# A hybrid decoder block on one core: activations stationary and weights moving in all large products

## The chip, the core and the metric

The kernel runs on one core of a Trainium2 chip, in one launch. The metric is device time in microseconds, the median of three runs: before 1590.8 us (1589.44 to 1592.45). Engines are named as the profile names them: PE is TensorE (PEld its loads of stationary operands), DVE VectorE, ACT ScalarE, POOL GpSimd, SP the engine that issues most transfers.

## The reference, cut to what matters

256 tokens, 2048 channels, float32. Six modulation vectors come from one matrix, the input is normalized and modulated, projected by one wide matrix, mixed by a gated delta rule (8 heads of 128) and by a convolution of width 31, merged by two sigmoid gates and projected out; then a gated MLP (5632 wide) with a convolution of width 3 on its gate.

```python
mod = silu(c) @ w_ada + b_ada                      # 2048 x 12288
sh1, sc1, gt1, sh2, sc2, gt2 = split(mod, 6)
hn = rmsnorm(x, norm1_g) * (1 + sc1) + sh1
proj = hn @ w_in                                   # qkv, z, beta, a, glu, gate_a, gate_b
a = delta_rule(silu(conv4(qkv)), beta, g) * silu(z) @ dn_w_o
b = silu(layernorm(conv31(val * sigmoid(gl)))) @ cf_w_o
x = x + gt1 * ((sigmoid(gate_a) * a + sigmoid(gate_b) * b) @ w_out)
hn = rmsnorm(x, norm2_g) * (1 + sc2) + sh2
gate, up = split(hn @ w_up, 2)
x = x + gt2 * ((silu(conv3(gate)) * up) @ w_down)
out = rmsnorm(x, final_norm_g)
```

## The kernel before

Channels lie on the partitions throughout: x is fed transposed, and `x_sb`, `hn`, `gb`, `ga`, `mg`, `res` are 16 row tiles of 128 channels by 256 tokens. All large products go through `product` (L257): for 512 outputs, two banks of sums, and for each pair of row tiles a weight chunk `w` of 2 x 128 x 512 (512 KB). ScalarE rounds it to a leading part `wh` (L267), VectorE makes the remainder `wl` (L269); activations are split the same way, and three matmuls make up one product: `wh` by the leading part (L280), `wh` by the rest (L281), `wl` by the leading part (L282). The weights are stationary in blocks of 128x128, the 256 tokens move: 24 matmuls a chunk. `w` has five buffers, `wh` and `wl` three. There are 488 chunks.

The order of products: `p1` (70 chunks: the first rows for q, k, v, GLU and a gate), the last rows of these, z, gate `ga`, the convolution branch's `cfo` (16), the delta branch's `dno` (16), `out` (32), `up1` (60: the first rows of six groups of the MLP), then the rest of gate and up, `down` (48), five more groups of gate and up, `down` (40).

The modulation vectors are side work (`ada_block`, L134). A step brings 384 or 512 KB of `w_ada` into `ada_w` and VectorE adds the rows, each times an entry of silu(c), to `ada_acc` (L155). A block of 8 or 16 steps ends with sums over the partitions (turns on TensorE, L172). `product` pulls steps as it issues chunks, `side_rate` of them per chunk; from L768 on `ada_w` has two buffers. `need` (L194) pulls all steps that are left of a block: the first output gate before `out` (L819), scale and shift of the second norm before `up1` (L829) and inside it (L840).

The order of instructions on an engine comes from a scheduler that simulates the program, with priorities in bands (`b_first` before `b_delta`, `b_w`, `b_main`, `b_ada`). Each engine then runs its list in order. PSUM: four banks `mm` for products, one `sm`, three (`dl`, `dl0`, `dl1`) for the delta rule and the rest. The delta rule's state `St` (L602) and Q of the first heads (L423) have buffers of their own.

Of the kernel before, what the change touches and what calls it, by code (L numbers as in the profile page):

```python
# [8 lines left out]
F32 = mybir.dt.float32  # L9
# [20 lines left out]
for _name, _w in (  # L30
    ("b_ada", 96), ("n1g", 16), ("n2g", 16), ("fg", 16), ("dnconv", 96), ("dng", 1),
    ("cfconv", 248), ("lng", 8), ("lnb", 8), ("ffconv", 132), ("c", 16),
):
    VEC[_name] = (_n, _w)
    _n += _w
# [3 lines left out]
class Band:  # L39
    """A run of scheduling priorities of its own."""  # L40
# [15 lines left out]
def block_kernel(ctx: ExitStack, tc, xT, vec, ab, w_ada, w_in, dn_w_o, cf_w_o, w_out, w_up, w_down, outT):  # L56
# [61 lines left out]
    R3, R2 = [(0, 4), (4, 10), (10, KD)], [(0, 8), (8, KD)]  # L118
    RANGES = [R3, R3, R2, R3, R3, R2]
    mod = [[p0.tile([P, k1 - k0], F32, name=f"mod{j}{k0}") for k0, k1 in RANGES[j]] for j in range(6)]  # L120
# [13 lines left out]
    def ada_block(j, part, pool, bufs, band=None, shared=False):  # L134
# [3 lines left out]
        acc = (pool if shared else p0).tile([P, n if shared else 1024], F32, tag="ada_acc", bufs=2 if shared else 1, name="ada_acc")  # L138
        c0 = j * D + k0 * P
        step = 2 if n <= 512 else 1  # L140
        if shared:
            pt = ps.tile([P, 512], F32, tag="sm", name="pt")
        for kc in range(0, KD, step):
            with band():
                wt = pool.tile([P, step, n], F32, tag="ada_w", bufs=bufs, name="ada_w")
                last_ada[0] = nc.sync.dma_start(out=wt, in_=av[:, kc:kc + step, c0:c0 + n]).ins
                for i in range(step):
# [4 lines left out]
                    elif k == 0:  # L152
# [3 lines left out]
            if kc + step < KD:  # L156
                yield
        with (b_delta if band is not nullcontext else nullcontext)():
            if band is nullcontext:
                if not shared:  # L160
                    pt = ps.tile([P, 512], F32, tag="sm", name="pt")
# [3 lines left out]
            else:  # L165
                # the sums over the partitions, with the channels turned to the partitions
                tot = p0.tile([P, nk], F32, tag="ada_t", name="ada_t")
                for i in range(0, nk, 4):
                    n4 = min(4, nk - i)
                    pt = ps.tile([P, 4, P], F32, tag="sm", name="pt")  # L170
# [33 lines left out]
    def sumsq_acc(acc, src, k, pt):  # L204
        """Adds src ** 2 / D over the channels to pt[:, c] for the tokens of chunk c, with most of the sums over the row tiles on the vector engine."""
        n = KD - 4
        sq = acc if k == 0 else p0.tile([P, 2, S], F32, tag="t2", bufs=2, name="sq1")[:, 0, :]
        nc.scalar.activation(out=sq, in_=src, func=AF.Square)
        if 0 < k < n:
            nc.vector.tensor_tensor(out=acc, in0=acc, in1=sq, op=ALU.add)  # L210
        if k >= n - 1:
            v = acc if k == n - 1 else sq
            for c in range(2):
                nc.tensor.matmul(pt[:, c:c + 1], lhsT=v[:, c * P:(c + 1) * P], rhs=ones_d, start=(k == n - 1 and c == 0), stop=(k == KD - 1), skip_group_check=True)
# [7 lines left out]
    def spread(a, pool=pd, tag="dl"):  # L222
        """a ** -0.5 of two columns, as rows on every partition."""
# [17 lines left out]
    def modulate(dst, src, A, sh, rs, part):  # L241
        """dst[:, 0] and dst[:, 1]: the leading part and the rest of src * A * rstd + sh."""
# [704 lines left out]
```

## Time and profile before

| | |
|---|---|
| median of three runs | 1590.8 us |
| span of the profiled execution | 1586.7 us |
| its instructions | 31357 |
| busy: TensorE, VectorE, ScalarE | 1545.4, 1188.0, 796.2 us |
| transfers | 366.25 MB, mean 231 GB/s |

The median is the time of an execution, the span lies inside it, from the first to the last instruction of the profile; what the profiled execution itself took beside its span is not recorded, and the two differ by 4.1 us. In the page, a duration of a matmul contains the time that it waits in the pipeline behind others: how far apart two starts lie (the pitch) says what a matmul costs in a stream. The chain of waits is read backwards from the last instruction. Windows give the busy time of each engine in a stretch, and the clock granted to TensorE there (1.00 is 2.4 GHz, 0.50 is 1.2 GHz).

### The profile page before, as it was taken

To read this page: it belongs to the slowest core of one execution; us is meant where nothing else is said; L and a number is where in the kernel's file an instruction comes from. 1 tells how busy PE (TensorE), PEld (TensorE's weight loads), DVE (VectorE), ACT (ScalarE), POOL (GpSimd) and SP (SyncE) were. 2 spreads that over 40 slices of the span, in tenths; PEclk is the share of its full clock that TensorE was granted. 3 is DMA by queue.
4 is the path that set the end of the run, shared out by engine and by line. 5 is a ranking of instruction groups with operands and counts; after the bars stand their busy time and mean duration, and the time that the engine had idled before them with its cause. 6 is when DMAs were issued, how large, how long until landed. Compare 5 with 4: busy or idle time off the path is not lost.

```text
span 1586.7 us, 31357 instructions
## 1 busy us (share of the span) xinstructions
PE 1545.4 (97%) x12818; PEld 1534.9 (97%) x12818; DVE 1188.0 (75%) x1566; ACT 796.2 (50%) x1232; POOL 51.7 (3%) x112
## 2 busy tenths in 40 slices
PE   6999999899999999999989999999999999999997
PEld 5999999899999999999979999999999999999997
DVE  5789967789889878897777889987444777655554
ACT  4554434766885584454446434555334444444443
POOL 2000000400020010000000000000000000000000
PEclk7999999999999999999989999999999999999998
DMA  9999866534456668889779998765556777665552
GB/s 346 384 335 349 266 185 174 159 107 131 122 155 218 199 192 303 305 271 340 254 241 305 308 307 305 216 183 184 187 189 224 244 253 262 190 185 185 187 187 94
DMA packets 186848, 366.25 MB, mean 231 GB/s; under 512 B 12496, under 2 KB 37072, under 8 KB 186704
## 3 DMA queue, kind: packets, MB, share of 16 engines
q1 hardware_dynamic: 186704, 364.26, 70.1%
q8 instruction: 100, 1.64, 0.4%
q14 instruction: 44, 0.36, 0.1%
HBM read 362.11 MB, written 2.10 MB: 230 GB/s over the span
## 4 chain that ended last, share of the span: by engine, by line
PE 86%; DMA 5%; DVE 3%; issue 2%; POOL 2%; ACT 1%; SPq 0%; DVEq 0%; POOLq 0%; ACTq 0%
PE mm_up L282 7%; PE mm_up L280 7%; PE mm_up L281 7%; PE mm_down L282 5%; PE mm_down L280 5%; PE mm_down L281 5%; DMA ada_w<-in_w_ada 5%; PE mm_p L282 4%; PE mm_p L281 4%; PE mm_p L280 4%; PE mm_gate L280 4%; PE mm_gate L281 4%; PE mm_gate L282 4%; PE mm_ga L282 2%; PE mm_ga L281 2%; PE mm_ga L280 2%
## 5 line engine op out<-in xcount | busy, mean ns | idle before, releaser
L267 ACT CAST wh<-w 128x1024 fp32r<-128x1024 f32 x488 | 511.4, 1049 | 631.0 <-PE mm_up L281 141.0
L269 DVE TENSOR_TENSOR wl<-w,wh 128x1024 fp32r<-128x1024 f32 x488 | 595.5, 1221 | 265.0 <-ACT wh L267 263.8
L155 DVE SCALAR_TENSOR_TENSOR ada_acc<-ada_w,c_act,ada_acc 128x768 f32<-128x768 f32 (+2 forms) x232 | 237.6, 1024 | 65.2 <-DMA ada_w<-in_w_ada 62.8
L280 PE MATMUL mm_up<-hn,wh 128*128 128x256 f32 x944 | 266.4, 285 | 1.7 <-ACT hn L251 1.7
L281 PE MATMUL mm_up<-hn,wh 128*128 128x256 f32 x944 | 267.4, 284 | 0.0
L282 PE MATMUL mm_up<-hn,wl 128*128 128x256 f32 x944 | 264.7, 284 | 0.2 <-DVE wl L269 0.2
L282 PE MATMUL mm_down<-h,wl 128*128 128x256 f32 x704 | 197.5, 281 | 0.0
L280 PE MATMUL mm_down<-h,wh 128*128 128x256 f32 x704 | 197.0, 280 | 0.0
L281 PE MATMUL mm_down<-h,wh 128*128 128x256 f32 x704 | 195.8, 278 | 0.0
L280 PEld LDWEIGHTS mm_up<-hn,wh 128*128 128x128 f32 x944 | 181.9, 193 | 2.0 <-ACT hn L251 2.0
L281 PEld LDWEIGHTS mm_up<-hn,wh 128*128 128x128 f32 x944 | 182.1, 193 | 0.0
L282 PEld LDWEIGHTS mm_up<-hn,wl 128*128 128x128 f32 x944 | 180.7, 193 | 0.4 <-DVE wl L269 0.4
L280 PE MATMUL mm_p<-hn,wh 128*128 128x256 f32 x560 | 157.1, 285 | 1.6 <-ACT hn L251 1.6
L281 PE MATMUL mm_p<-hn,wh 128*128 128x256 f32 x560 | 157.7, 285 | 0.3 <-DVE hn L252 0.3
L282 PE MATMUL mm_p<-hn,wl 128*128 128x256 f32 x560 | 153.1, 286 | 0.1
L281 PEld LDWEIGHTS mm_down<-h,wh 128*128 128x128 f32 x704 | 132.4, 188 | 0.0
L280 PEld LDWEIGHTS mm_down<-h,wh 128*128 128x128 f32 x704 | 132.4, 188 | 0.0
L282 PEld LDWEIGHTS mm_down<-h,wl 128*128 128x128 f32 x704 | 132.1, 188 | 0.0
L281 PE MATMUL mm_gate<-hn,wh 128*128 128x256 f32 x464 | 131.0, 283 | 0.0
L280 PE MATMUL mm_gate<-hn,wh 128*128 128x256 f32 x464 | 130.9, 283 | 0.0
L282 PE MATMUL mm_gate<-hn,wl 128*128 128x256 f32 x464 | 129.7, 283 | 0.0
L280 PEld LDWEIGHTS mm_p<-hn,wh 128*128 128x128 f32 x560 | 108.2, 194 | 1.6 <-ACT hn L251 1.6
(301 smaller groups left out, 3334.0 us busy)
## 6 DMA issues: line engine op xcount, KB each, us to landing
w<-in_w_up SPq DMA_DIRECT2D x176, 512.0 KB, 4.4
w<-in_w_in SPq DMA_DIRECT2D x130, 512.0 KB, 3.9
ada_w<-in_w_ada SPq DMA_DIRECT2D x96, 512.0 KB, 5.2
ada_w<-in_w_ada SPq DMA_DIRECT2D x128, 384.0 KB, 5.2
w<-in_w_down SPq DMA_DIRECT2D x88, 512.0 KB, 3.7
w<-in_w_in SPq DMA_DIRECT2D x64, 256.0 KB, 4.1
w<-in_w_out SPq DMA_DIRECT2D x32, 512.0 KB, 5.1
w<-in_cf_w_o SPq DMA_DIRECT2D x16, 512.0 KB, 5.3
```

The costliest lines, as they stand in the source:

```text
L155: nc.vector.scalar_tensor_tensor(out=acc[:, 0:n], in0=wt[:, i, :], scalar=c_act[:, k:k + 1], in1=acc[:, 0:n], op0=ALU.mult, op1=ALU.add)
L267: nc.scalar.copy(out=wh, in_=w)
L269: nc.vector.tensor_tensor(out=wl, in0=w, in1=wh.bitcast(F32), op=ALU.subtract)
L280: nc.tensor.matmul(o, lhsT=wh[:, kk, cs], rhs=xh(k), start=(k == k0 and j % 2 == 0), stop=False, skip_group_check=True)
L281: nc.tensor.matmul(o, lhsT=wh[:, kk, cs], rhs=xl(k), start=False, stop=False, skip_group_check=True)
L282: nc.tensor.matmul(o, lhsT=wl[:, kk, cs], rhs=xh(k), start=False, stop=(k == k1 - 1), skip_group_check=True)
```

## The change

In `product` the activations become the stationary operand, 128 tokens at a time, and 512 columns of a weight chunk move: 12 matmuls a chunk. Sums then lie with tokens on the partitions, [128 tokens, 512 outputs] in each of two banks. Where channels must be on the partitions (convolutions, merged branches, normalized input, the MLP's hidden values) a new helper `turned` transposes two row tiles by four turns into a bank of tag `tp` (two banks). x and the output are no longer transposed outside; norms sum squares along a row on ScalarE (`add_to_res`, `rstd_col`). The two output gates become rows on all partitions, by a matmul with ones (`as_row`); their bias comes in as a row by a transfer, after a clearing on POOL. Q of the first heads (`conv00`) and the state `St` move into the buffers of `ada_w`. Cut to its core, with the removed code of the evictions left out:

```diff
-    ps = ctx.enter_context(tc.tile_pool(name="ps", bufs=1, space=bass.MemoryType.PSUM))
+    ps = ctx.enter_context(tc.tile_pool(name="ps", bufs=2, space=bass.MemoryType.PSUM))
...
+        as_row = j in (2, 5)
+        if as_row:
+            with (b_delta if band is not nullcontext else nullcontext)():
+                nc.gpsimd.memset(acc, 0.0)
+                r0 = (j == 5) * D + k0 * P
+                nc.sync.dma_start(out=acc[0:1, 0:n], in_=rowv[:, r0:r0 + n])
...
+        if as_row:
+            with b_delta():
+                for i in range(0, n, 512):
+                    pt = ps.tile([P, 512], F32, tag="tp", name="pt")
+                    nc.tensor.matmul(pt, lhsT=ones, rhs=acc[:, i:i + 512], start=True, stop=True)
+                    nc.scalar.copy(out=gt_row(j, (k0 * P + i) // 512), in_=pt)
+            ready.add((j, part))
+            yield
+            return
...
+    def rstd_col(ss):
+        a = p0.tile([P, 2], F32, tag="nrm_a", name="nrm_a")
+        nc.vector.tensor_reduce(out=a, in_=ss, axis=mybir.AxisListType.X, op=ALU.add)
+        nc.gpsimd.tensor_scalar(out=a, in0=a, scalar1=1.0 / D, scalar2=EPS, op0=ALU.mult, op1=ALU.add)
+        r = p0.tile([P, 2], F32, tag="nrm_c", bufs=3, name="nrm_c")
+        nc.gpsimd.tensor_tensor(out=r, in0=a, in1=mhalf[:, 0:2], op=ALU.pow)
+        return r
...
+    def turned(src, tiles, pool=ps, tag="tp"):
+        bank = pool.tile([P, 2, S], F32, tag=tag, name="turned")
+        for i, j in enumerate(tiles):
+            for t in range(2):
+                turn(bank[:, i, t * P:(t + 1) * P], src[:, t, j * P:(j + 1) * P])
+        return bank
...
-            order = [(kk, j) for kk in range(2) for j in range(4)] if kc + 2 < k1 else [(kk, j) for j in range(4) for kk in range(2)]
-            for kk, j in order:
+            order = [(kk, t) for kk in range(2) for t in range(2)] if kc + 2 < k1 else [(kk, t) for t in range(2) for kk in range(2)]
+            for kk, t in order:
                 k = kc + kk
-                o = pts[j // 2][:, j % 2, :]
-                cs = slice(j * P, (j + 1) * P)
-                nc.tensor.matmul(o, lhsT=wh[:, kk, cs], rhs=xh(k), start=(k == k0 and j % 2 == 0), stop=False, skip_group_check=True)
-                nc.tensor.matmul(o, lhsT=wh[:, kk, cs], rhs=xl(k), start=False, stop=False, skip_group_check=True)
-                nc.tensor.matmul(o, lhsT=wl[:, kk, cs], rhs=xh(k), start=False, stop=(k == k1 - 1), skip_group_check=True)
+                ts = slice(t * P, (t + 1) * P)
+                nc.tensor.matmul(pts[t], lhsT=xh(k)[:, ts], rhs=wh[:, kk, :], start=(k == k0), stop=False)
+                nc.tensor.matmul(pts[t], lhsT=xl(k)[:, ts], rhs=wh[:, kk, :], start=False, stop=False)
+                nc.tensor.matmul(pts[t], lhsT=xh(k)[:, ts], rhs=wl[:, kk, :], start=False, stop=(k == k1 - 1))
         evac(pts)
...
+            into(gls[g], True)(pts)
+            bank = ps.tile([P, 2, S], F32, tag="tp", name="turned")
+            for t in range(2):
+                v = gls[g][t]
+                nc.scalar.activation(out=v[:, S:], in_=v[:, S:], func=AF.Sigmoid)
+                nc.vector.tensor_tensor(out=v[:, 0:S], in0=v[:, 0:S], in1=v[:, S:], op=ALU.mult)
+                for i in range(2):
+                    turn(bank[:, i, t * P:(t + 1) * P], v[:, i * P:(i + 1) * P])
+            nc.scalar.copy(out=us[g][:, :, CFK - 1:], in_=bank)
...
+                into(both(src), True)(pts)
+                if hb + i:
+                    dst = p1.tile([P, 4, S], F32, tag=SLOTS[hb * 3 + i], name=f"conv{hb}{i}")
+                else:
+                    dst = p0.tile([P, 4, S], F32, tag="ada_w", bufs=2, name="conv00")
                 out.append(dst)
+                for h in range(2):
+                    bank = turned(src, (2 * h, 2 * h + 1))
+                    for u in range(2):
+                        j = 2 * h + u
+                        n = (i * 8 + hb * 4 + j) * 4
+                        nc.scalar.activation(out=dst[:, j, :], in_=bank[:, u, :], func=AF.Copy, scale=V("dnconv", n + 3))
+                        for sft in (1, 2, 3):
+                            nc.vector.scalar_tensor_tensor(
+                                out=dst[:, j, sft:], in0=bank[:, u, 0:S - sft], scalar=V("dnconv", n + 3 - sft), in1=dst[:, j, sft:], op0=ALU.mult, op1=ALU.add)
...
-                St = pq.tile([P, 4, P], F32, tag="St", name="St")
+                St = p0.tile([P, 4, P], F32, tag="ada_w", bufs=2, name="St")
...
+            for pt, a, b in zip(pts, both(ga, g), both(gb, g)):
+                nc.vector.tensor_tensor(out=a, in0=pt, in1=a, op=ALU.mult)
+                nc.vector.tensor_tensor(out=b, in0=a, in1=b, op=ALU.add)
+            for k in (4 * g, 4 * g + 2):
+                bank = turned(gb, (k, k + 1))
+                nc.scalar.copy(out=mg[:, 0, k:k + 2, :], in_=bank)
+                nc.vector.tensor_tensor(out=mg[:, 1, k:k + 2, :], in0=bank, in1=mg[:, 0, k:k + 2, :].bitcast(F32), op=ALU.subtract)
...
-        nc.sync.dma_start(out=res[:, 4 * q:4 * q + 4, :], in_=xv[:, 4 * q:4 * q + 4, :])
+    res = p0.tile([P, 2, D], F32, tag="x", name="res")
+    for t in range(2):
+        for q in range(2):
+            nc.sync.dma_start(out=res[:, t, q * 1024:(q + 1) * 1024], in_=xv[:, t, q * 1024:(q + 1) * 1024])
...
+    def add_to_res(j, g, ss):
+        def evac(pts):
+            with b_first():
+                for t in range(2):
+                    r = both(res, g)[t]
+                    tmp = p0.tile([P, 512], F32, tag="t2", bufs=2, name="tmp")
+                    nc.vector.tensor_tensor(out=tmp, in0=pts[t], in1=gt_row(j, g), op=ALU.mult)
+                    nc.vector.tensor_tensor(out=r, in0=tmp, in1=r, op=ALU.add)
+                    nc.scalar.activation(out=tmp, in_=r, func=AF.Square, accum_out=ss[:, t, g:g + 1])
+        return evac
     for g in range(4):
...
-        product("out", rows(w_out, 512 * g), whole, lambda k: mg[:, 0, k, :], lambda k: mg[:, 1, k, :], evac)
+        product("out", rows(w_out, 512 * g), whole, lambda k: mg[:, 0, k, :], lambda k: mg[:, 1, k, :], add_to_res(2, g, ss2))
...
+    def modulate2(part):
+        k0, k1 = R3[part]
+        with b_first():
+            xn = p2.tile([P, 2, (k1 - k0) * P], F32, tag="raw", name="xn")
+            nc.scalar.activation(out=xn[:, 0, :], in_=res[:, 0, k0 * P:k1 * P], func=AF.Copy, scale=r2[:, 0:1])
+            nc.vector.tensor_scalar(out=xn[:, 1, :], in0=res[:, 1, k0 * P:k1 * P], scalar1=r2[:, 1:2], scalar2=None, op0=ALU.mult)
+            for k in range(0, k1 - k0, 2):
+                bank = turned(xn, (k, k + 1), pd, f"dl{k // 2 % 2}")
+                for i in range(2):
+                    c = slice(k + i, k + i + 1)
+                    split(hn2, k0 + k + i, bank[:, i, :], A2[part][:, c], mod[3][part][:, c])
...
+            def whole_sums(pts, g, i):
+                if g < NG:
+                    into(both(pre[2 * g + i]), True)(pts)
+                    return pre[2 * g + i]
+                t = p2.tile([P, 2, 512], F32, tag=f"h5{i}", name="sums")
+                into(both(t), False)(pts)
+                return t
             def evac_gate(pts, g=g, sg=sg):
+                src = whole_sums(pts, g, 0)
+                for h in range(2):
+                    bank = turned(src, (2 * h, 2 * h + 1))
+                    for u in range(2):
+                        j = 2 * h + u
+                        n = (4 * g + j) * 3
+                        nc.scalar.activation(out=sg[:, j, :], in_=bank[:, u, :], func=AF.Copy, scale=V("ffconv", n + 2))
+                        for sft in (1, 2):
+                            nc.vector.scalar_tensor_tensor(
+                                out=sg[:, j, sft:], in0=bank[:, u, 0:S - sft], scalar=V("ffconv", n + 2 - sft), in1=sg[:, j, sft:], op0=ALU.mult, op1=ALU.add)
                 nc.scalar.activation(out=sg, in_=sg, func=AF.Silu)
             def evac_up(pts, g=g, sg=sg):
+                src = whole_sums(pts, g, 1)
+                for h in range(2):
+                    bank = turned(src, (2 * h, 2 * h + 1), pd, f"dl{h}")
+                    s2 = sg[:, 2 * h:2 * h + 2, :]
+                    nc.vector.tensor_tensor(out=s2, in0=bank, in1=s2, op=ALU.mult)
```

VectorE, before, while the convolution of width 31 (`cfa`) and the delta rule run (the rows begin at the 137th weight remainder, and the first step of width 1024 comes after the 128th): steps of the first output gate (`ada_acc`, width 1024) stand singly between the remainders (`wl`).

```order
L269 TENSOR_TENSOR wl<-w,wh 128x1024
L401 SCALAR_TENSOR_TENSOR cfa_4459<-u_355,vt,cfa_4459 128x256 x2
L155 SCALAR_TENSOR_TENSOR ada_acc<-ada_w,c_act,ada_acc 128x1024
L401 SCALAR_TENSOR_TENSOR cfa_4459<-u_355,vt,cfa_4459 128x256 x2
L269 TENSOR_TENSOR wl<-w,wh 128x1024
L539 COPY_PREDICATED U_5019<-mi_101,bank 128x64x4
L398 TENSOR_TENSOR cfa_4459<-cfa_4459,prod 128x512
L155 SCALAR_TENSOR_TENSOR ada_acc<-ada_w,c_act,ada_acc 128x1024
L401 SCALAR_TENSOR_TENSOR cfa_4459<-u_355,vt,cfa_4459 128x256 x2
L539 COPY_PREDICATED U_4971<-mi_107,bank 128x32x8
L269 TENSOR_TENSOR wl<-w,wh 128x1024
L401 SCALAR_TENSOR_TENSOR cfa_4459<-u_355,vt,cfa_4459 128x256 x2
```

After, the first of these steps comes after the 177th remainder; from the 181st on:

```order
L295 TENSOR_TENSOR wl<-w,wh 128x1024
L166 SCALAR_TENSOR_TENSOR ada_acc<-ada_w,c_act,ada_acc 128x1024
L643 SCALAR_TENSOR_TENSOR N_4230<-bank,eg,N_4230 128x128 x4
L668 SCALAR_TENSOR_TENSOR ol_4846<-bank,vt,oh_4845 128x4x128
L166 SCALAR_TENSOR_TENSOR ada_acc<-ada_w,c_act,ada_acc 128x1024
L668 SCALAR_TENSOR_TENSOR ol_4846<-bank,vt,oh_4845 128x4x128
L166 SCALAR_TENSOR_TENSOR ada_acc<-ada_w,c_act,ada_acc 128x1024
L668 SCALAR_TENSOR_TENSOR ol_4864<-bank,vt,oh_4863 128x4x128
L662 TENSOR_TENSOR on<-on,z_4696 128x512
L166 SCALAR_TENSOR_TENSOR ada_acc<-ada_w,c_act,ada_acc 128x1024 x3
L295 TENSOR_TENSOR wl<-w,wh 128x1024 x2
L166 SCALAR_TENSOR_TENSOR ada_acc<-ada_w,c_act,ada_acc 128x1024
```

Steps that stood singly among remainders, over the products of `ga` and `cfo`, now stand six together before the next two remainders, beside the last work of the delta rule (`N`) and its output (`ol`).

SP, after, with what each transfer waits for, at the end of the conv-branch weights: the first transfers of modulation weights.

```order
L291 DMA w<-in_dn_w_o 128x2x512 [waits DMAHW5_49,DVE_49]
L291 DMA w<-in_dn_w_o 128x2x512 [waits DMAHW6_49,DVE_49]
L291 DMA w<-in_dn_w_o 128x2x512 [waits DMAHW7_49,DVE_49]
L157 DMA ada_w<-in_w_ada 128x1024 [waits PE_49]
L291 DMA w<-in_dn_w_o 128x2x512 [waits DMAHW0_49,DVE_49]
L157 DMA ada_w<-in_w_ada 128x1024 [waits DMAHW5_49,DVE_49]
L291 DMA w<-in_dn_w_o 128x2x512 [waits DMAHW1_49,DVE_49]
L291 DMA w<-in_dn_w_o 128x2x512 [waits DMAHW2_49,DVE_49]
L157 DMA ada_w<-in_w_ada 128x1024 [waits DMAHW7_49,DVE_49]
L291 DMA w<-in_dn_w_o 128x2x512 [waits DMAHW3_49,DVE_49]
L157 DMA ada_w<-in_w_ada 128x1024 [waits DMAHW4_49,DMAHW2_49,DVE_49]
L291 DMA w<-in_dn_w_o 128x2x512 [waits DVE_49]
```

The first waits for TensorE's last read of what lay in that buffer; the next three wait for VectorE and lie between weight transfers that wait for VectorE too. Before, these transfers stood among the weights of `ga` and `cfo`.

TensorE, after, at the start of the out product (`pt<-ada_acc,ones` makes the gate's rows, `turned<-ident,gb` turns the merged branches):

```order
L306 MATMUL mm_dno<-wh,ol_4864 128x512
L307 MATMUL mm_dno<-wl,oh_4863 128x512
L174 MATMUL pt<-ada_acc,ones 128x512 x2
L86 MATMUL turned<-ident,gb 128x128 x8
L305 MATMUL mm_out<-wh,mg 128x512 x2
L86 MATMUL turned<-ident,gb 128x128 x4
L306 MATMUL mm_out<-wh,mg 128x512
L307 MATMUL mm_out<-wl,mg 128x512
```

The rows of the gate stand before the first turns and the first matmul of `out`, and wait for the last step of the gate's second block; before, the turns of the gate's sums stood beside the products.

## Rows read from the trace of the kernel before

**Rows 1.** The page: busy time of the engines; granted clock in 40 slices, in tenths.

```profile
PE 1545.4 (97%) x12818; PEld 1534.9 (97%) x12818; DVE 1188.0 (75%) x1566; ACT 796.2 (50%) x1232; POOL 51.7 (3%) x112
...
PEclk7999999999999999999989999999999999999998
```

**Rows 2.** The page: the chain that ended last, by engine and by line.

```profile
PE 86%; DMA 5%; DVE 3%; issue 2%; POOL 2%; ACT 1%; SPq 0%; DVEq 0%; POOLq 0%; ACTq 0%
PE mm_up L282 7%; PE mm_up L280 7%; PE mm_up L281 7%; PE mm_down L282 5%; PE mm_down L280 5%; PE mm_down L281 5%; DMA ada_w<-in_w_ada 5%; PE mm_p L282 4%; PE mm_p L281 4%; PE mm_p L280 4%; PE mm_gate L280 4%; PE mm_gate L281 4%; PE mm_gate L282 4%; PE mm_ga L282 2%; PE mm_ga L281 2%; PE mm_ga L280 2%
```

**Rows 3.** Timeline of TensorE, first down product: start, duration, engine, line (eight starts apart).

```profile
1199.63 0.28 PE L280 MATMUL mm_down<-h,wh 128*128 128x256 f32 x1
...
1200.57 0.28 PE L282 MATMUL mm_down<-h,wl 128*128 128x256 f32 x1
```

**Rows 4.** The same at 40 us, at half clock (seven starts apart).

```profile
40.15 0.41 PE L280 MATMUL mm_p<-hn,wh 128*128 128x256 f32 x1
...
41.64 0.41 PE L282 MATMUL mm_p<-hn,wl 128*128 128x256 f32 x1
```

**Rows 5.** Windows: window, length, busy us (count) of PE PEld DVE ACT POOL, clock, DMA.

```profile
40.00:42.00 2.00, 2.00 (x11) 2.00 (x11) 2.00 (x5) 0.69 (x1) 0.00 (x0) 0.50 1.04 372
120.00:160.00 40.00, 39.88 (x332) 39.58 (x331) 38.83 (x49) 17.00 (x21) 0.00 (x0) 1.00 0.98 351
801.00:816.00 15.00, 9.96 (x53) 8.91 (x52) 11.66 (x24) 4.89 (x10) 0.70 (x1) 0.66 0.77 252
840.00:880.00 40.00, 40.00 (x336) 40.00 (x335) 33.26 (x40) 23.57 (x35) 0.00 (x0) 1.00 0.92 302
1160.00:1200.00 40.00, 40.00 (x342) 40.00 (x342) 17.15 (x14) 16.66 (x18) 0.00 (x0) 1.00 0.58 186
```

**Rows 6.** Chain in order of time: transposes (L86) and fp32 matmuls (L729); start, us.

```profile
5.28 4.95 PE bank L86 x20
...
548.84 1.06 PE pt L729 x4
...
800.78 0.22 PE pt L86 x2
```

**Rows 7.** The same chain from 610 us.

```profile
610.13 5.54 DMA ada_w<-in_w_ada
615.76 1.30 DVE ada_acc L155
617.07 4.71 DMA ada_w<-in_w_ada
621.87 1.30 DVE ada_acc L155
623.18 5.49 DMA ada_w<-in_w_ada
```

**Rows 8.** VectorE by line and shape: count, busy us, mean ns, idle time before.

```profile
L269 DVE TENSOR_TENSOR wl<-w,wh 128x1024 fp32r<-128x1024 f32 x488 | 595.5, 1221 | 265.0 <-ACT wh L267 263.8 <-DMA ada_w<-in_w_ada 0.5
...
L155 DVE SCALAR_TENSOR_TENSOR ada_acc<-ada_w,c_act,ada_acc 128x1024 f32<-128x1024 f32 x60 | 76.8, 1281 | 18.1 <-DMA ada_w<-in_w_ada 17.9
...
L155 DVE SCALAR_TENSOR_TENSOR ada_acc<-ada_w,c_act,ada_acc 128x512 f32<-128x512 f32 x52 | 39.0, 750 | 10.1 <-DMA ada_w<-in_w_ada 9.3
```

**Rows 9.** The page's DMA issues: count, KB each, us from issue to landing.

```profile
ada_w<-in_w_ada SPq DMA_DIRECT2D x96, 512.0 KB, 5.2
...
w<-in_w_down SPq DMA_DIRECT2D x88, 512.0 KB, 3.7
```

**Rows 10.** By tile: conv-branch and out product; ns min/median/max, first and last start.

```profile
L280 PE MATMUL mm_cfo<-cfh,wh x128: 277/280/367, 610.1 to 658.2; 128*128 128x256 f32 x128
...
L282 PE MATMUL mm_out<-mg,wl x256: 278/283/370, 706.0 to 801.4; 128*128 128x256 f32 x128
```

**Rows 11.** What line 155 of VectorE waited for: us, times.

```profile
  DMA ada_w<-in_w_ada: 62.8, 70
```

More of the change, by code (lines that the diff above doesn't have):

```diff
@@ L259, in product @@
         k0, k1 = ks
[L260 removed]
+        pts = [pm.tile([P, 512], F32, tag="mm", name=f"mm_{label}") for _ in range(2)]
         for kc in range(k0, k1, 2):
@@ L350, in into, with both @@
         return evac
-    def pairs(t):
-        return [t[:, 0:2, :], t[:, 2:4, :]]
-    early = [(qkv_src(hb, i), pairs(qkvt[hb][i])) for hb in range(2) for i in range(3)]
-    early += [(glu_src(g), [us[g][:, :, CFK - 1:], gls[g]]) for g in range(4)]
-    early += [(rows(w_in, C_GB + 512 * g), pairs(gb[:, 4 * g:4 * g + 4, :])) for g in range(4)]
+    def both(t, g=0):
+        return [t[:, i, 512 * g:512 * (g + 1)] for i in range(2)]
+    early = [(qkv_src(hb, i), both(qkvt[hb][i])) for hb in range(2) for i in range(3)]
+    early += [(glu_src(g), gls[g]) for g in range(4)]
+    early += [(rows(w_in, C_GB + 512 * g), both(gb, g)) for g in range(4)]
     for g in range(4):
@@ L406, in evac @@
             def evac(pts, g=g):
-                for i in range(2):
-                    d = dst[:, 4 * g + 2 * i:4 * g + 2 * i + 2, :]
+                for d, pt in zip(both(dst, g), pts):
                     if add:
-                        into([d], True)(pts[i:i + 1])
-                    nc.scalar.activation(out=d, in_=d if add else pts[i], func=AF.Sigmoid)
+                        into([d], True)([pt])
+                    nc.scalar.activation(out=d, in_=d if add else pt, func=AF.Sigmoid)
             product(label, rows(w_in, c0 + 512 * g), ks, hh, hl, evac)
@@ L783, in evac @@
         def evac(pts, g=g):
-            for i in range(2):
-                d = gb[:, 4 * g + 2 * i:4 * g + 2 * i + 2, :]
-                nc.vector.tensor_tensor(out=d, in0=pts[i], in1=d, op=ALU.mult)
+            for d, pt in zip(both(gb, g), pts):
+                nc.vector.tensor_tensor(out=d, in0=pt, in1=d, op=ALU.mult)
         product("cfo", rows(cf_w_o, 512 * g), half8, lambda k: cfs[k // 2][0][:, k % 2, :], lambda k: cfs[k // 2][1][:, k % 2, :], evac)
@@ L890, in block_kernel @@
         for g in range(4):
             def evac(pts, g=g):
+                add_to_res(5, g, ss3)(pts)
                 with b_first():
[L893 to L898 removed]
+                    for r in both(res, g):
+                        nc.vector.tensor_tensor(out=r, in0=r, in1=fg_row[:, 512 * g:512 * (g + 1)], op=ALU.mult)
@@ new lines, in block_kernel @@
+    ov = out.rearrange("(t p) n -> p t n", p=P)
+    for g in range(4):
+        for t in range(2):
+            cs = slice(512 * g, 512 * (g + 1))
+            if t == 0:
+                nc.scalar.activation(out=res[:, t, cs], in_=res[:, t, cs], func=AF.Copy, scale=r3[:, t:t + 1])
+            else:
+                nc.vector.tensor_scalar(out=res[:, t, cs], in0=res[:, t, cs], scalar1=r3[:, t:t + 1], scalar2=None, op0=ALU.mult)
+            nc.sync.dma_start(out=ov[:, t, cs], in_=res[:, t, cs])
```

232 lines of the change are left out of this document (88 added, 144 removed).

## The prediction

> **What bounds the kernel now.** I read the page first: TensorE busy 97% of 1586.7 us, VectorE 75%, the granted clock at full in nearly every slice [rows 1]. The page's chain of work agrees: 86% of the span is TensorE, all of it in the large products, and 5% the transfer of modulation weights [rows 2]. So time is TensorE's instructions times their pitch, except where that transfer ends last.
>
> Then the pitch. In the first down product eight starts lie 0.94 us apart, 117 ns each [rows 3]. By windows without a gap it is 40/342 us = 117 ns there and 40/336 = 119 ns in the up product [rows 5]; most products are of the second kind, I take 118.5. Each matmul has 256 moving columns, 106.7 ns at 2.4 GHz, so about 11 ns are not columns. At the half clock (0.50 in the window 40 to 42 us [rows 5]) seven starts lie 1.49 us apart, 213 ns [rows 4]: that is 256 columns at 1.2 GHz with nothing left over. What costs the 11 ns at full clock is therefore no fixed number of TensorE cycles; the load of stationary weights, which each matmul has, is hidden if columns take 213 ns.
>
> Last, the chain at 610 us, the one stage where a transfer bounds: 5 us of transfer, 1.3 us of VectorE step, and again [rows 7]. The two sum to about 6.5 us (13.05 us for two), and with two buffers it is a step in 3.3 us.
>
> **The large products.** A weight chunk (488 of them [rows 8]) has 24 matmuls of 256 columns before and 12 of 512 after. Before: 11,712 x 118.5 ns = 1388 us. After: 5,856 at 213.3 ns (columns alone, as the half-clock rows have it) up to 213.3 + 11 = 224 ns (the present excess kept per instruction). I take 215, by the half-clock rows: 1259 us. **-129 us.**
>
> **Added and removed on TensorE.** Results now have tokens on partitions, and where channels must be there they are turned: 304 transposes of 128x128 (GLU 16, q/k/v 48, merged 32, second norm 32, gate and up sums 176). Two in a stream of matmuls took 0.22 us [rows 6], so 304 x 0.11 = **+33**. Two output gates become rows by eight fp32 matmuls of 512 columns; four instructions of 256 took 1.06 us [rows 6], so 16 of 512 take **+8**. Away go 32 transposes of gate sums, 40 instructions of sums of squares and 12 of the spread of 1/rms: 84 x 0.11 = **-9**. TensorE together: -97 us.
>
> The price of a transpose has another end. At the start, on an engine that had been idle, twenty took 4.95 us, 0.25 each [rows 6]; at that price 304 cost 43 us more. I take the lower, since all but a few lie between large matmuls. The Trainium skill ("TensorE: Matmul & The Clock Gate", section "Part 4: PE-mode transpose") speaks against the change more strongly: about 275 ns in one kernel's context, by which the sum would be 50 us higher (an estimate from that page). This trace's 0.11 us in the stream does not agree with it.
>
> **What the order shows: the modulation waits.** The block of the first output gate (32 steps of 128x1024) and those of the next scale and shift (16 steps) hold the out product and the second norm. Before, VectorE does the first of them after its 128th weight remainder and the 48 are spread over some 78 chunks. Now Q of the first heads and a state of the delta rule lie in the two buffers of the modulation weights. The first transfer is queued on SP behind 181 weight chunks, the first step stands after the 177th remainder, the last of the 48 before the 207th, and the first four steps go through one buffer, each transfer waiting for the step before it. VectorE runs in order and the remainders of later chunks stand behind these steps; TensorE has no more than three chunks of reserve. What is queued behind the wait: remainders, hence matmuls, hence evictions.
>
> The stretch, step by step. Four steps through one buffer: 6.5 us each [rows 7] = 26. Twenty-eight of 128x1024 through two: lone, a 512 KB transfer lands in 3.7 us (as the down weights do [rows 9]), plus a step of 1.28 [rows 8], halved 2.5 us; contended 3.3 [rows 7]. I take 3.0, between, since weight chunks and four reloads of the input (2 MB) share the queue but stop when their buffers are full: 84. Sixteen with two halves of 0.75 us each [rows 8]: (3.7 + 1.5)/2 = 2.6 to (5.2 + 1.5)/2 = 3.35 [rows 9], I take 2.9: 46. Turnover of the blocks and the reloads: 4. Together 160 us. TensorE's own work there: 29 chunks x 12 x 0.215 = 75, with transposes, gate rows and the end of the delta rule 85. So it stands 75 us; before, from 610 us to the end of the out product at 801.4 [rows 10], it stood about 4 in the same steps. **+71 us.** Ends: all lone (4 x 5.0 + 70 + 42 = 132) gives +43; all contended with 8 us of turnover (26 + 92 + 54 + 8 = 180) gives +91.
>
> **Three smaller terms.** After the 9 us gap before the up product TensorE came back at half clock, 0.66 granted over 801 to 816 us [rows 5]; some 5 us at half speed lose 2.5 us of work. I count two such restarts behind the new gap: **+5** (0 to 10). In the early products (70 chunks) and the first up products (60) modulation steps run beside them: VectorE has 38.83 of 40 us at 120 to 160 [rows 5], so a faster TensorE gains nothing there; at 840 to 880 it has 33.26 and follows. A chunk gives 24 x 118.5 - 12 x 215 = 0.26 us, 130 chunks 34 us; I leave a fifth uncollected, **+7** (0 to 34). Head (input now turned on chip, norm by columns instead of spread rows) and tail (no spread, scale split over two engines): no row shows either whole; they replace like with like, 0 (-5 to +5). VectorE's evictions keep their widths; the two-step gate (multiply, add) replaces one wide step and the adds of squares, cover for both is the product running beside them.
>
> **Sum.** 1586.7 - 97 + 71 + 5 + 7 = 1572.7 us of span. Around the span lie 1590.8 - 1586.7 = 4.1 us if the profiled execution was the median one, so **1576 us** against 1590.8, about 1% less. The gain on TensorE is sure within its pitch; two thirds of it go back to a wait that was covered before. With ends of the wait and of the smaller terms, this case has 1545 to 1598.
>
> **Rivals.**
> 1. The wait is hidden: transfers run ahead (buffers free earlier than I read it), TensorE keeps its cover. For it: before, 62.8 us of waiting for this transfer on VectorE [rows 11] cost TensorE little. Against it: VectorE now has the steps bunched, twelve in a row without one remainder between. It leaves out 71 and 5: 1500 us.
> 2. On the slower side: the modulation keeps the contended pace. Place: the same stretch; price: 180 in place of 160 us, +20, 1596 us. It decides from 174 us on (1590.8 - 1576 = 15 over 160), a mean step near (174 - 30)/44 = 3.3 us, which is just what the chain shows at 610 us [rows 7]. Against it: there the weight chunks came at full rate, here they stop.
> 3. A 512-column matmul keeps the fixed 11 ns: 9 ns more on about 5,000 instructions outside the stretch, +45, 1621 us. Against it the half-clock rows [rows 4].
> 4. A transpose costs what the start shows, since each bank must be evicted before it is used again and TensorE waits for that: 0.25 us [rows 6], +43, 1619 us. Against it: two banks and a product between most groups.
>
> That the change doesn't do what it says is excluded by the order: each chunk has 12 matmuls.
>
> **Chances.** Forecast 0.55, rival 1 0.12, rival 2 0.20, rival 3 0.08, rival 4 0.05. A measurement of this kernel tells 0.2% (3.2 us) from no change. Faster: 0.50 of the forecast's 0.55 and rival 1, 0.62. Same: what lies near 1590.8 of forecast and rival 2, 0.07. Slower: 0.31. The range for 8 in 10 leaves out rival 1 and little above: 1532 to 1622 us.
>
> **What would show it.** Right: pitch of the large matmuls near 215 ns; 304 transposes at about 0.11; a stretch of some 75 us idle on TensorE between the conv-branch product and the out product, ended by the modulation's steps, with granted clock falling in it; chain of waits with modulation weights at 9% or more in place of 5%. Wrong: that idle stretch under 40 or over 100 us, a pitch of 220 ns or more, TensorE waiting for evictions of turned banks, or VectorE's remainders ending last through all early products.

## The result and the profile after

The changed kernel takes 1653.4 us (median of four runs, 1652.25 to 1656.46), the kernel before 1590.1 beside it: ratio 1.040 [1.038, 1.043], 4% slower. The forecast was 1576, its range ended at 1622.

The page after, busy time of the engines and granted clock in 40 slices (span 1654.8 us, to set beside [rows 1]):

```profile
PE 1530.3 (92%) x7198; PEld 1257.5 (76%) x7198; DVE 1192.5 (72%) x1556; ACT 811.3 (49%) x1223; POOL 56.4 (3%) x116
...
PEclk9999999999999999957999999999999999999998
```

The span grew by 68.1 us. TensorE's idle time (span less busy) went from 41.3 to 124.5 us, +83; its busy time from 1545.4 to 1530.3, only -15. The forecast had +78 of idle (71 and 7) and -92 of busy (-97 and 5). The wait came out near its size; the gain that was to outweigh it did not.

Windows after: window, length, busy us (count) of PE PEld DVE ACT POOL, clock, DMA share, GB/s:

```profile
640.00:680.00 40.00, 30.50 (x123) 24.26 (x122) 31.91 (x36) 13.99 (x24) 1.40 (x3) 0.87 0.74 237
720.00:760.00 40.00, 12.97 (x50) 8.74 (x51) 21.22 (x23) 5.59 (x8) 0.00 (x0) 0.62 0.61 190
640.00:880.00 240.00, 160.97 (x674) 126.84 (x673) 171.21 (x201) 73.86 (x114) 3.25 (x6) 0.84 0.77 256
```

And before, the stretch with the same stages:

```profile
600.00:840.00 240.00, 230.29 (x1893) 227.82 (x1892) 190.45 (x234) 105.11 (x150) 0.70 (x1) 0.98 0.85 289
```

240 - 160.97 = 79.0 us of idle against 9.7 before. The longest waits of TensorE there, in brackets, are these; and under them the steps of line 166 (line 155 before) of the three vectors concerned:

```profile
746.34 3.78 PE L174 MATMUL pt<-ada_acc,ones 128*128 128x512 f32 x4 [44.29 <-DVE ada_acc L166]
773.67 1.09 PE L86 MATMUL pt<-ident,ada_acc 128*128 128x128 f32 x4 [9.22 <-DVE ada_acc L166]
873.22 1.97 PE L86 MATMUL turned<-ident,xn 128*128 128x128 f32 x8 [10.98 <-ACT xn L877]
```

```profile
L166 DVE SCALAR_TENSOR_TENSOR ada_acc<-ada_w,c_act,ada_acc x62: 743/1276/1287, 627.0 to 799.9; 128x1024 f32<-128x1024 f32 x32, 128x512 f32<-128x512 f32 x30
627.00:801.00 174.00, 107.70 (x456) 84.47 (x455) 120.73 (x141) 49.35 (x79) 3.62 (x6) 0.80 0.74 241
```

53.5 us of the 79.0 end with a step of the modulation. 11.0 are the wait for the second norm's input (its waits came to 5.0 before), 6.4 are for weight remainders (2.6 before), 5.6 for the last of the delta rule. The 48 steps are 32 of width 1024 and 16 that add two rows of width 512 each; of these 32 rows the view has 30, since the first of each vector is only multiplied and not added. The steps run from 627.0 to 801 us, 174 us where the forecast had 160, and TensorE is idle for 174 - 107.7 = 66.3 of them.

Now the pitch, from TensorE's timeline after (start, duration, engine, line): in the delta branch's product at half clock four distances between starts make 1.71 us, in the up product at full clock five make 1.14 us, in down ten make 2.34 us. The window over the first of them shows its clock, 0.50.

```profile
649.99 0.63 PE L305 MATMUL mm_dno<-wh,oh 128*128 128x512 f32 x1
...
651.70 0.42 PE L306 MATMUL mm_dno<-wh,ol 128*128 128x512 f32 x1
...
649.90:651.70 1.80, 1.80 (x6) 1.32 (x5) 1.43 (x2) 1.33 (x5) 0.00 (x0) 0.50 0.17 68
...
900.30 0.39 PE L305 MATMUL mm_up<-wh,hn 128*128 128x512 f32 x1
...
901.44 0.39 PE L307 MATMUL mm_up<-wl,hn 128*128 128x512 f32 x1
...
1219.61 0.40 PE L305 MATMUL mm_down<-wh,h 128*128 128x512 f32 x1
...
1221.95 0.40 PE L305 MATMUL mm_down<-wh,h 128*128 128x512 f32 x1
```

That is 427, 228 and 234 ns. At half clock it is 512 columns at 1.2 GHz with nothing over, as with 256 in [rows 4]. At full clock 13 to 15 or 21 ns stand over the 213.3 ns of the columns. Over all products of the traces the mean distance of two starts, without single long ones, is 227 ns where `hn` or `mg` is stationary (227 to 230 in the early products) and 234 where `h`, `cfh` or `oh` is; before it was 120 and 117. With these, the large products cost 4416 x 0.227 + 1440 x 0.234 = 1339 us, 80 more than the forecast's 1259, and before them 8832 x 0.120 + 2880 x 0.1173 = 1398. By pitch they gained 59 us, where -129 was forecast.

The transposes did what was said. In the chain of waits six take 0.66 us:

```profile
1065.71 0.66 PE turned L86 x6
```

### The profile page after: what moved, and what is told of

The parts are those of the page before. It is cut to its first block, busy times and chain, and to the rows that moved or that the text cites. A ratio compares the mean times of both kernels' runs of the same rounds, so it can differ in the third digit from the quotient of the medians.

```text
span 1654.8 us, 20112 instructions
## 1 busy us (share of the span) xinstructions
PE 1530.3 (92%) x7198; PEld 1257.5 (76%) x7198; DVE 1192.5 (72%) x1556; ACT 811.3 (49%) x1223; POOL 56.4 (3%) x116
## 5 line engine op out<-in xcount | busy, mean ns | idle before, releaser
L305 PE MATMUL mm_up<-wh,hn 128*128 128x512 f32 x472 | 185.7, 396 | 0.2 <-ACT hn L263 0.2
L306 PE MATMUL mm_up<-wh,hn 128*128 128x512 f32 x472 | 185.3, 393 | 0.0
L307 PE MATMUL mm_up<-wl,hn 128*128 128x512 f32 x472 | 172.9, 395 | 5.4 <-DVE wl L295 5.2
L305 PE MATMUL mm_down<-wh,h 128*128 128x512 f32 x352 | 139.9, 397 | 0.0
L306 PE MATMUL mm_down<-wh,h 128*128 128x512 f32 x352 | 139.7, 397 | 0.0
L307 PE MATMUL mm_down<-wl,h 128*128 128x512 f32 x352 | 126.4, 397 | 0.0
L305 PE MATMUL mm_p<-wh,hn 128*128 128x512 f32 x280 | 109.7, 395 | 2.1 <-ACT hn L263 2.0
L307 PEld LDWEIGHTS mm_up<-wl,hn 128*128 128x128 f32 x472 | 88.2, 188 | 27.4 <-DVE wl L295 9.4
L306 PE MATMUL mm_p<-wh,hn 128*128 128x512 f32 x280 | 109.0, 391 | 0.0
L305 PEld LDWEIGHTS mm_up<-wh,hn 128*128 128x128 f32 x472 | 89.1, 189 | 18.6 <-ACT hn L263 0.6
L306 PEld LDWEIGHTS mm_up<-wh,hn 128*128 128x128 f32 x472 | 88.7, 188 | 18.3 <-issue 0.5
L307 PE MATMUL mm_p<-wl,hn 128*128 128x512 f32 x280 | 98.7, 393 | 0.9 <-DVE wl L295 0.9
L305 PE MATMUL mm_gate<-wh,hn 128*128 128x512 f32 x232 | 91.3, 394 | 0.0
L306 PE MATMUL mm_gate<-wh,hn 128*128 128x512 f32 x232 | 90.6, 391 | 0.0
L307 PEld LDWEIGHTS mm_down<-wl,h 128*128 128x128 f32 x352 | 66.4, 189 | 16.1
L306 PEld LDWEIGHTS mm_down<-wh,h 128*128 128x128 f32 x352 | 66.4, 189 | 15.9
L305 PEld LDWEIGHTS mm_down<-wh,h 128*128 128x128 f32 x352 | 66.4, 189 | 15.8
```

Source lines behind the costliest of these rows:

```text
L305: nc.tensor.matmul(pts[t], lhsT=xh(k)[:, ts], rhs=wh[:, kk, :], start=(k == k0), stop=False)
L306: nc.tensor.matmul(pts[t], lhsT=xl(k)[:, ts], rhs=wh[:, kk, :], start=False, stop=False)
L307: nc.tensor.matmul(pts[t], lhsT=xh(k)[:, ts], rhs=wl[:, kk, :], start=False, stop=(k == k1 - 1))
```

## The experiments

Two questions: what holds the modulation back, and what sets the pitch. "Theory 1" in the expectations is a fixed cost per matmul at full clock.

**The state out of the modulation's buffers.** The forecast blamed "Q of the first heads and a state". In the trace after, the state is written twice by ScalarE, the second time late, and read until 640 us:

```profile
L641 PE MATMUL bank<-St,conv x16: 271/275/377, 473.6 to 640.2; 128*128 128x128 f32 x16
L637 ACT COPY St<-bank x2: 585/586/587, 452.2 to 623.5; 128x512 f32<-128x512 f32 x2
```

So only the state was moved out.

```diff
-                St = p0.tile([P, 4, P], F32, tag="ada_w", bufs=2, name="St")
+                St = pq.tile([P, 4, P], F32, tag="T0", name="St")
```

> The changed kernel with one line put back: the delta rule's state St has a buffer of its own (the tag of a dead tile), Q of the first heads stays in the buffers of the modulation weights. The order then has the first modulation step of the first output gate after the 129th remainder (177th in the changed kernel, 128th before). Theory (two causes that add: the wait for modulation weights, and a pitch of 227 to 234 ns): TensorE stood about 79 us between 640 and 880 us and stood 9 in the same products before, so 70 us go, 1653 - 70 = 1583 us, pitch unchanged. Rival (the modulation's steps only move their wait to other places, since VectorE has less to spare beside the products of ga and cfo): less than half of it comes back, 1620 us or more.

1581.7 us (1578.09 to 1586.67), ratio 0.995 [0.993, 0.997] to before: 72 us less than after, and 0.5% under before. Its page, its window of that stretch, and line 166:

```profile
PE 1525.2 (97%) x7198; PEld 1254.1 (79%) x7198; DVE 1188.5 (75%) x1556; ACT 808.9 (51%) x1220; POOL 56.9 (4%) x116
```

```profile
600.00:840.00 240.00, 224.24 (x1005) 179.93 (x1004) 189.76 (x230) 110.62 (x172) 7.38 (x8) 0.97 0.85 284
```

```profile
L166 DVE SCALAR_TENSOR_TENSOR ada_acc<-ada_w,c_act,ada_acc x49: 740/1279/1286, 446.8 to 688.6; 128x1024 f32<-128x1024 f32 x32, 128x512 f32<-128x512 f32 x17
```

The steps start at 446.8 us in place of 627.0, and the idle time of the stretch is 15.8 us in place of 79.0; 9.7 of the 15.8 are the second norm's wait, which stays. The expected 1583 came.

**The same sharing in the kernel before.** Is it sharing, or the late start?

```diff
-                dst = (p1 if hb + i else pq).tile([P, 4, S], F32, tag=SLOTS[hb * 3 + i], name=f"conv{hb}{i}")
+                dst = p1.tile([P, 4, S], F32, tag=SLOTS[hb * 3 + i], name=f"conv{hb}{i}") if hb + i else p0.tile([P, 4, S], F32, tag="ada_w", bufs=2, name="conv00")
...
-                St = pq.tile([P, 4, P], F32, tag="St", name="St")
+                St = p0.tile([P, 4, P], F32, tag="ada_w", bufs=2, name="St")
```

> The kernel before with only the sharing: Q of the first heads and the state St in the two buffers of the modulation weights, products unchanged. Its order has the first step after the 151st remainder and the last of the 48 after the 208th, 57 chunks apart against 30 in the changed kernel. Theory (what costs is the late start and not the sharing as such; the delta rule ends later in the changed kernel's order): 48 steps in 57 x 2.84 = 162 us at some 3.2 us each just fit, 1590 to 1605 us. Rival (the sharing itself costs what the changed kernel lost): 1660 us.

1592.6 us, ratio 1.002 [1.000, 1.003]. Line 155:

```profile
L155 DVE SCALAR_TENSOR_TENSOR ada_acc<-ada_w,c_act,ada_acc x39: 745/1284/1287, 574.1 to 718.1; 128x1024 f32<-128x1024 f32 x30, 128x512 f32<-128x512 f32 x9
```

The steps of this row start at 574.1 us (475.6 before), and that is still early enough. So sharing as such costs nearly nothing. In both kernels that share, the first step follows closely on the second copy of the state: at 627.0 us after 623.5 in the changed kernel, here at 569.6 (a first multiply, which the row leaves out) after 565.9. That fits transfers that come in order behind the second state in their buffers; no run shows this apart from the order of the queue. And that copy is late in the changed kernel even with the state apart: 612.0 us, against 564.3 before. So a late delta rule with the state apart, or the sharing with an early one, costs little; the two together cost 72 us. Why the delta rule ends later in the changed kernel stays open.

**What sets the pitch.** In the kernel with the state apart, the late products get other operands (`still` and `moved`) and widths (`cut`). What they sum is then something else than the reference; only their pitch is read.

```diff
+                        nc.tensor.matmul(pts[t][:, c:c + cut], lhsT=ss[n], rhs=mm[n][:, c:c + cut], start=(k == k0 and n == 0 and c == 0), stop=(k == k1 - 1 and n == 2), skip_group_check=True)
...
+            cut = {8: 256, 10: 128}.get(g, 512)
...
+                still, moved = ((None, None), ((nh, nl), None), ("w", None), (None, mn))[g]
...
+            still, moved = ((None, mh), ((nh, nl), mn), ((nh, nl), mh), (None, None))[g]
```

> The kernel of e1 with other operands in the down products and other widths in some gate and up products; the down products then compute something else than the reference. Widths with hn stationary: 512 (gate, up), 2 x 256 (gateb, upb), 4 x 128 (gatec, upc). Theory 1 (a fixed 13 ns beside N columns at 2.4 GHz): 227, 120 and 67 ns. Theory 2 (columns at 2.2 per ns whatever the width): 227, 114, 57 ns. With h stationary 234 for 512 and 117 for 256 (downh). Places, all with 512 columns: downa h stationary and weights moving (234 as in the changed kernel), downb hn and weights, downc weights and weights, downd h and hn, downe h and h, downf hn and hn, downg hn and h. Theory P (it is the place of the stationary tile): downb, downf, downg 227, downa, downd, downe 234. Theory M (it is something of the down products, the same weights or sums): all 234. Theory X (stationary and moving in one place cost each other): downa 234 differs from downe, downf.

Mean distance of two starts at full clock, in ns, worked out from its trace:

| stationary, moving | 512 columns | 256 | 128 |
|---|---|---|---|
| hn, weights | 226.7 | 119.9 | 111.7 |
| h, weights | 234.3 | 118.7 | |
| weights, weights | 227.9 | | |
| h, h | 227.6 | | |
| hn, hn | 227.0 | | |
| h, hn | 234.1 | | |
| hn, h | 233.4 | | |

Two rows of tiles show the two prices (ns min/median/max of a duration, first and last start; the names put the moving operand first): 120 matmuls in 27.1 and in 27.8 us.

```profile
L313 PE MATMUL mm_downf<-hn x120: 387/389/398, 1523.6 to 1550.7; 128*128 128x512 f32 x120
L313 PE MATMUL mm_downg<-h,hn x120: 392/394/402, 1550.9 to 1578.7; 128*128 128x512 f32 x120
```

213.3 + 13.3 and 106.7 + 13.3: with `hn` the excess is the same 13.3 ns at both widths, so fixed per matmul between these two widths: theory 1, and not theory 2, which had 114 for 256. At 128 columns the expected sum failed: 111 ns is about what a transpose takes. With that the sum of theory 1 holds at 256 and 512 columns only. The extra 7 ns belong to no tile, so theories P and M fall: operands of one tile are cheap, of two tiles sometimes dear.

**The tiles laid out otherwise.** First uses at the front of the pool give `hn` another address.

```diff
+    for tag, shape, dt_, n in (("x", [P, 2, D], F32, 1), ("t2", [P, 2, S], F32, 2), ("w", [P, 2, 512], F32, 5), ("wh", [P, 2, 512], F32R, 3), ("wl", [P, 2, 512], F32R, 3), ("ada_acc", [P, 1024], F32, 1), ("ada_w", [P, 1024], F32, 2)):
+        first = p0.tile(shape, dt_, tag=tag, bufs=n, name=f"first_{tag}")
...
+        nc.gpsimd.memset(v8 if dt_ == F32 else v8.bitcast(F32), 0.0)
```

> The kernel of e1 with the tiles of the first pool in another order, nothing else: hn (and mg, hn2 in its slot) at bytes 101600 to 134368 of a partition instead of 40160 to 72928, wh and wl at 63936 to 88512 instead of 97504 to 122080; the tiles h, cfh, oh stay above 153920. Seven tiny clearings on POOL are added. Theory B (a border at byte 131072: stationary and moving operand on either side of it cost 234 in place of 227 ns): only the rest of hn's rows 13 to 15 (the last of the slot) reads at 234, all else as in e1, time within 3 us of e1's 1582. Theory N (it goes with which tile lies higher, the stationary or the moving one): all products with hn read at 234, 4416 x 7 ns = 31 us more, 1613 us. Theory 0 (something else of the tile h): no pitch changes at all.

1603.0 us in its one run. The `hn` products rise to 233 ns: in the up product 13 distances make 3.03 us.

```profile
949.73 0.40 PE L309 MATMUL mm_up<-wh,hn 128*128 128x512 f32 x1
...
952.76 0.40 PE L309 MATMUL mm_up<-wh,hn 128*128 128x512 f32 x1
```

The time is nearest to theory N's, but N falls by the row "hn, h" above, and the border theory and theory 0 fall as well. What fits all seven rows and this kernel is where the two operands begin in a partition, modulo 256 bytes, by the addresses that the expectations give: equal (224 and 224) costs 227, different (64 and 224, here 224 and 192) 233 to 234.

**That offset swept.** The stationary operand begins n bytes later, within `hn`; the sums are again something else than the reference.

```diff
...
+                    a = k % 15 * S + t * P + off
+                    sh, sl = (hn2[:, i, :, :].rearrange("p k s -> p (k s)")[:, a:a + P] for i in range(2))
...
```

> The kernel of e1 with other stationary operands in eight down products and in the gate and up products of the last five groups: 128 columns of hn that begin a few columns later, so what they sum is something else than the reference. Theory R (what decides between 227 and 234 is where the stationary operand begins against where the moving one begins, counted in a partition's bytes modulo 256; in all runs so far equal gave 227 and other gave 232 to 235): with 512 columns, onea (0 bytes later) 227, oneb to oneh (16, 32, 64, 96, 128, 160, 224 later) 232 to 235; with 2 x 256, twoa (0) and twoj (256) 120, twob to twoi (16, 32, 64, 96, 128, 160, 192, 224) 117 to 119. Rival (it goes with the tile itself): all at 227 and 120.

| bytes later | 0 | 16 | 32 | 64 | 96 | 128 | 160 | 192 | 224 | 256 |
|---|---|---|---|---|---|---|---|---|---|---|
| 512 columns, ns | 227.1 | 226.7 | 233.3 | 233.4 | 234.2 | 233.4 | 233.4 | | 233.4 | |
| 256 columns, ns | 120.0 | 118.3 | 118.3 | 114.6 | 118.7 | 119.2 | 120.0 | 114.0 | 116.7 | 120.0 |

Tiles at 16 and 32 bytes (each 142 distances, 32.2 and 33.1 us), then windows with 256 columns at 0 and 192:

```profile
L312 PE MATMUL mm_oneb<-wh,hn x96: 389/389/390, 1119.9 to 1152.1; 128*128 128x512 f32 x96
L312 PE MATMUL mm_onec<-wh,hn x96: 392/395/397, 1152.6 to 1185.7; 128*128 128x512 f32 x96
```

```profile
1222.00:1240.00 18.00, 18.00 (x152) 18.00 (x151) 9.78 (x9) 6.41 (x7) 0.00 (x0) 1.00 0.76 241
1389.00:1407.00 18.00, 18.00 (x160) 18.00 (x160) 11.09 (x15) 9.22 (x12) 0.00 (x0) 1.00 0.64 186
```

All this is one tile, so the offset is the cause and not the tile. 256 bytes cost what 0 does, at the one width that tried it. 16 bytes were expected to be dear and were not. And offset 0, cheap at 512 columns, is among the dearest at 256, where 64, 192 and 160 bytes missed the expected 117 to 119.

**Offsets made equal in the new kernel.** 160 unused bytes make `h`, `cfh` and `oh` begin at 224 as the weights do.

```diff
+    pad = p0.tile([P, 40], F32, name="pad")
+    nc.gpsimd.memset(pad, 0.0)
```

> The kernel of e1 with an unused tile of 160 bytes at the end of the first pool, and a clearing of it: h, cfh, cfl, oh, ol, which began at 64 modulo 256, now begin at 224 as hn, wh and wl do. Theory R: the pitch of the conv-branch, delta-branch and down products falls from 234 to 227, 1440 x 7.5 ns = 11 us, 1582 - 11 = 1571 us. Rival (it goes with the tile): no change, 1582 us.

1574.4 us (1573.24 to 1578.82), ratio 0.991 [0.990, 0.993]: 7.3 us under the kernel with the state apart, of the 11 expected. The intervals of the two ratios just touch, but the pitch moved clear of noise: the down product falls from 234 to 227 ns (eight distances in 1.81 us), the conv and delta branch to 228 to 230.

```profile
1149.69 0.39 PE L306 MATMUL mm_down<-wh,h 128*128 128x512 f32 x1
...
1151.50 0.39 PE L306 MATMUL mm_down<-wh,h 128*128 128x512 f32 x1
```

**Offsets changed in the kernel before,** first by 160 bytes behind `hn` (the diff is that of above, in the first pool), then by 64 there (`[P, 16]`) and 32 more at the end of the pool `p0` (`[P, 8]`).

> The kernel before with the same unused tile of 160 bytes right behind hn: wh and wl, which began at 64 modulo 256 as hn did, now begin at 224; h and the other tiles move with them. Theory R: with 256 moving columns equal beginnings cost 120 ns and others 117 to 118, so 8832 matmuls x 2 to 2.5 ns = 18 to 22 us less, 1570 us. Rival: no change, 1590 us.

1588.9 us, ratio 1.000 [0.999, 1.001]: no gain, where 1570 was expected. The distances of the `hn` products now scatter from 116 to 125 around the same 120, as the sweep has it at 160.

> The kernel before with two unused tiles (64 bytes behind hn, 32 at the end of the first pool), products unchanged: wh and wl now begin 64 bytes after hn, and h, cfh, cfl, oh, ol 64 after them, modulo 256. Theory R as the sweep of e6 corrects it (equal or 16 bytes apart 227 for 512; for 256 columns the distance decides, 120 at 0 and 160, 118 at 32, 114 at 64 and 192), taken over to weights stationary and activations moving: 8832 matmuls from 120 to 114.3 and 2880 from 117.3 to 114.3, 59 us less on TensorE; some 10 to 20 of them not collected where VectorE and the modulation's transfers are near their limit: 1540 to 1552 us. Rival (the sweep does not hold with the roles exchanged): 1590 us, as e8.

1559.5 us (1555.55 to 1564.2), ratio 0.981 [0.979, 0.983]: the fastest kernel here that computes the reference, 5.7% under the changed one (1559.46/1653.43) and the direction of the expectation, not its size. A window of the late gate and up products in it and, under it, in the kernel before:

```profile
1040.00:1080.00 40.00, 40.00 (x354) 40.00 (x353) 37.39 (x56) 24.65 (x31) 0.00 (x0) 1.00 0.58 193
```

```profile
1040.00:1080.00 40.00, 40.00 (x336) 40.00 (x335) 36.09 (x52) 23.26 (x30) 0.00 (x0) 1.00 0.62 188
```

`hn` and `mg` products average 115.6 ns (119.9 before), a mixture of 113 to 114 and 117 to 119; the down products stay at 117.8 (117.7 before), though they too begin 64 bytes apart (there the moving operand is the later one, 192 in the sweep's count).

**Without the transposes behind the head.** The kernel with the state apart, where 304 of 336 turns are left out and plain slices of the same shape are read instead; what follows is then something else than the reference. The cut at the end of the diff is the same for GLU.

```diff
+        if started:
+            flat = src.rearrange("p t n -> p (t n)")[:, tiles[0] * S:(tiles[0] + 2) * S]
+            return flat.rearrange("p (u s) -> p u s", u=2)
...
```

> The kernel of e1 without the 304 transposes behind the head: the evictions read the sums as they lie in SBUF, so what is computed from them is something else than the reference; all other instructions stay. Theory (a transpose costs what the stream shows, 0.11 us, and the few waits of TensorE beside them, 10 us in e1's trace): 1582 - 33 - 5 to 10 = 1540 to 1545 us. Rival (the turns cost little, since VectorE and the modulation's transfers bound the stages in which they stand): 1560 to 1575 us.

1559.6 us (1554.77 to 1560.94), ratio 0.981 [0.978, 0.984]: 22 us less than with them. The expected 1540 to 1545 missed, the time is at the near end of the rival's 1560 to 1575.

```profile
PE 1491.1 (96%) x6894; PEld 1225.0 (79%) x6894; DVE 1187.5 (76%) x1556; ACT 802.1 (51%) x1220; POOL 60.8 (4%) x116
```

TensorE is busy 34.1 us less, 0.112 for each of the 304; idle time rises by 11.6 (54.8 to 66.4), so a third of this gain is not collected. It goes in small waits: from the kernel with the turns to this one, TensorE's wait for one step of POOL rises from 0.9 to 5.4 us, that for the second norm's result from 9.7 to 12.0, those for weight remainders from 9.4 to 12.0 in all.

## Why the prediction was wrong

**The step that failed** is in the first part: "What costs the 11 ns at full clock is therefore no fixed number of TensorE cycles; the load of stationary weights, which each matmul has, is hidden if columns take 213 ns", and from it "I take 215, by the half-clock rows". The rows were read rightly: at half clock nothing is left over. But that says nothing on full clock, where the excess stood in every row of before. With operands that begin alike it is there 13.3 ns per matmul at 256 and at 512 columns. Wider matmuls save one excess of two, 4416 x 13.3 ns = 59 us, and the 1440 whose operands begin apart (64 and 224) save nothing (2 x 117.3 = 234.6 against 234). 59 is 70 us short of 129; the forecast of 1576 and these 70 make 1646, and the result is 1653. The 7 that are left are the sum of what the wait and the smaller terms were off by. What in TensorE takes the 13.3 ns no run shows.

**The range failed with it.** Its end of 1622 us lies by rival 3's 1621, where the pitch is 224 ns, "the present excess kept per instruction", a bound from before's mean. 227 to 234 lies above that, since before's mean mixed two prices and the new layout gave 1440 of the instructions the dear one. Rival 3 had the mechanism, at 0.08, and a size of 45 us; it was the one to weigh, being what the full-clock rows show by themselves. The narrower 1545 to 1598 was also added up too tightly: the forecast's own upper ends (wait +20, restarts +5, uncollected gain +27, head and tail +5) reach 1633 if all come out.

The Trainium skill ("TensorE: Matmul & The Clock Gate", section "Wait — 56ns, not 53.3ns?") says that at the warm clock a start follows after N/2.4 ns and some 2.5 ns more, which cold does not show. That the excess shows only at full clock agrees with the 427 ns above; its size does not: 13.3 to 21 ns here.

**The wait** (+71, "stands 75 us") came where it was placed: up to the end of the out product TensorE stood 69.6 us against 4.7 before, +65, and putting the state elsewhere gave 72 us back. Rival 1, that it hides, is out. But the size is in part luck, since two sizes were off and cancel. The 48 steps took 174 us, not 160, the time from which rival 2, at 0.20, was to decide: its pace came. And beside them TensorE had 107.7 us of work, not 85: one chunk more than the 29 that were counted, some 6 us by the dearer pitch and 9 by the half clock. So it stood 66.3 us in the stretch, neither 75 nor rival 2's 95. The second norm's wait, 11.0 us against 5.0, had no term.

**Transposes** at 0.11 (+33): 0.112, so rival 4 is out. In time they cost 22.

**Smaller terms.** Idle time outside the 240 us rose by 13.9 us (45.5 against 31.6), 7 were counted. Busy time makes -59 + 33 + 8 - 9 + 5 = -22 by the terms, with 5 for restarts, where -15 was measured. If each matmul is given the time up to the next start, the large products take 1374.4 us of it after and 1417.9 before, so -43.5 and not -59. Some 10 of the difference are single distances over a tenth longer than the pitch, at full clock (22.9 us in all, 12.8 before); what lengthens them no run took apart. The head's small instructions take 23.5 us against 23.4, the tail's some 3 less. Half clock is not the reason either. In the stretch it costs 11.1 us of work, half of the 22.2 that TensorE is busy at 1.2 GHz there, against 3.4 at the restart before, so +8 where +5 was counted; but before, the stretch from 17 to 44 us was at half clock too and cost 9.9, and after it is not.

**Signs named beforehand:** the idle stretch, its main cause (53.5 us of it) and its falling clock came; "a pitch of 220 ns or more" was the sign of a wrong forecast, and came. The chain's share of modulation weights can't be read for it: after, the chain reaches back only to 872 us.

## What to carry to other kernels

An excess that vanishes at half clock isn't thereby hidden at full clock: take the pitch from rows at the clock in which the time is spent, and carry what stands over the columns along per instruction. Before a long-lived tile joins the buffers of a stream, look at what is fetched through them next and when its last reader runs: with an early last reader it cost 3 us here, with a late one 72. And when a matmul stream has an excess, try where its two operands begin before rewriting it: 96 unused bytes gave 1.9%, the whole change without its wait 0.5%.

## What the runs showed of the hardware

The pitch depends on how the beginnings of the stationary and the moving operand in their partitions stand to each other. At 512 columns 0 and 16 bytes cost 227 ns, the six other offsets tried 233 to 234; at 256 columns 64 and 192 cost 114 to 115, and 0, 160 and 256 cost 120. Why the cheap offsets differ by width, why one product mixes 113 and 118 ns, and why the down products gained nothing at 64 stays open.
